# A convolution stage with ten of its sixteen blocks on TensorE, delayed copies through memory, grouped statistics, and a layer norm whose steps stand in one order

## The chip, the core and the metric

One core of a Trainium2 chip runs one program. Its engines are TensorE (PE, with its weight loads shown apart as PEld), VectorE (DVE), ScalarE (ACT), GpSimd (POOL) and SyncE (SP), each with an instruction stream of its own, and 16 DMA engines that serve the DMA queues of SP, ACT and POOL. The metric is the device time of one execution in microseconds (us), where less is better.

## The reference

A trunk of two layers (DEPTH 2, width 2048, 256 frames, float32). Each layer has a token mixer (layer 0: the Conformer convolution module, layer 1: gated linear attention) and a gated feed-forward network with a short convolution. The modulations come from a vector c by a projection. The change touches the start and layer 0's mixer:

```python
mod = (c_act @ ada_w[i] + ada_b[i]).reshape(B, N_MOD, 1, D)
h = _rms_norm(x, norm_g[i, 0]) * (1.0 + scale_m) + shift_m

def _conv_module(h, w_in, dw_w, dw_b, ln_g, ln_b, w_out):
    a, gate = jnp.split(h @ w_in, 2, axis=-1)
    z = _causal_dwconv(a * jax.nn.sigmoid(gate), dw_w, dw_b)   # CONV_WIDTH = 31 taps
    z = jax.nn.silu(_layer_norm(z, ln_g, ln_b))                # over the 2048 channels
    return z @ w_out

x = x + gate_m * _rms_norm(y, norm_g[i, 1])
```

## The kernel before

**Layout.** Channels stand on partitions, in 16 blocks of 128, and the 256 frames in the free direction; the projections into a mixer yield this layout. cout, the projection out of the mixer, yields tokens on partitions, in four columns (c) of 512 channels, from four weight tiles each. Every weight tile is 128 x 2048 (1 MB). SP loads the tiles in one list (`items`), which sets the order of the loads; `Stream` splits each into a high half on ACT (hi, L121) and a low half on DVE (lo, L123), in pieces of 1024, and three matmuls make one product: hi with the activation's high half, hi with its low half, lo with its high half (L756 to L758 in cin, L522 to L524 in cout).

**The projections of c.** adaLN tiles lie in the same list, of two kinds. For a "col" (in_adac, in_adah) PE multiplies c's columns with the tile (L364), DVE transposes the sums (L371), and PE (L378) and DVE (L381) finish. For a "row" (in_adar) DVE multiplies the tile with `cb`, a broadcast of silu(c), and sums along the row in one instruction (L350, 128 x 2048; a second small one reads the sum). `COLS_CONV`, `COLS_COUT` and `ROWS_COUT` say how many of them stand at each place of the program.

**Order.** The instructions of each engine are issued in an order that a scheduler settles at build time from the program's order and its priorities (`tc.high_priority`); `tc.issue_after` ties an instruction behind another one. An engine runs its list in that order, and so does each queue that issues DMAs.

**cin and gating.** The projection yields a and gate of a block side by side. `gather` adds the partial sums (L665) and multiplies by the sigmoid (L668 on ACT, L671 on DVE). The result zp is a block's input for the convolution.

**The convolution** starts as blocks come out of cin and goes on behind it. There are two routes. On DVE (`taps_dve`, eight blocks, two at a time) ACT makes the first tap and DVE thirty more, each a multiply-add over what is left of the frames (L685). On TensorE (`taps_pe`, the blocks in `PE_BLOCKS`) channels are split into four groups of 32. For each group an array of 128 partitions holds the 32 channels at four delays (zr): ACT copies zp behind 32 zeros (L708), PE makes each array by four matmuls with an identity (ps_late, L713), ACT copies it (L715). Then eight steps of four matmuls side by side (L730) sum all 32 delays, four at a time, by shifted views of zr and diagonal weights zt. DVE writes the first half of zt in one instruction (L724), ACT the second in 16 (L728). ACT evacuates with the bias (L733).

**Statistics.** PE sums each block over channels by a matmul with ones (`mean_add`, acc_m, L644). After twelve blocks (NA) their mean is taken as an estimate (mean_a); DVE subtracts it from each block (L631), ACT squares, PE sums (acc_v, L633). The last four are corrected for.

**Layer norm and cout.** r_ln is formed (L783 to L786: variance, clamp, root on ACT, reciprocal), every block has mu subtracted (L789), is multiplied by r_ln (L792), goes through ACT with gain, bias and Silu (L793) and is split into uc (ACT L424, DVE L425). cout (L522 to L524) multiplies these with weights; DVE multiplies the result by the gate (y, L583). The gate reaches its rows through memory: POOL's queue writes modulation columns out element by element (row<-m, L508) and reads them back as broadcast rows (gs, L512).

## Time and profile before

| what | us |
|---|---|
| median of 3 runs | 2376.75 |
| their range | 2374.56 to 2379.02 |
| the profiled execution | 2376.87 |
| its span | 2375.2 |
| first cin matmul | 29.6 |
| last gating of the convolution's input | 266.5 |
| variance (r_ln) formed | 352.4 |
| first cout matmul | 368.8 |
| last cout matmul | 463.0 |

All places in time are counted from the start of the span. The page gives busy time by engine, by line and by slices, and a chain of waits that is followed back from the last instruction. In the rows below, `L685 DVE ... out<-in ... x151 | 58.9, 460 | 0.0` reads: line of the kernel, engine, operation, tiles, shape, count, then busy us and mean ns of one, then idle time ahead of them and what ended it. TensorE's float32 matmuls leave two records for one instruction.

### The profile page before, as it was taken

To read this page: it belongs to the slowest core of one execution; us is meant where nothing else is said; L and a number is where in the kernel's file an instruction comes from. 1 tells how busy PE (TensorE), PEld (TensorE's weight loads), DVE (VectorE), ACT (ScalarE), POOL (GpSimd) and SP (SyncE) were. 2 spreads that over 40 slices of the span, in tenths; PEclk is the share of its full clock that TensorE was granted. 3 is DMA by queue.
4 is the path that set the end of the run, shared out by engine and by line. 5 is a ranking of instruction groups with operands and counts; after the bars stand their busy time and mean duration, and the time that the engine had idled before them with its cause. 6 is when DMAs were issued, how large, how long until landed. Compare 5 with 4: busy or idle time off the path is not lost.

```text
span 2375.2 us, 34238 instructions
## 1 busy us (share of the span) xinstructions
PE 2318.7 (98%) x13516; PEld 1955.8 (82%) x13516; DVE 1772.2 (75%) x2554; ACT 1212.4 (51%) x1909; POOL 16.8 (1%) x43
## 2 busy tenths in 40 slices
PE   6999998999999999999999999999999999999998
PEld 5888746788878888888878888888888888888886
DVE  3779998778878888888877877756887466645665
ACT  5334465555534554345565576655554455544543
POOL 0000000000000000000000000000000000000000
PEclk9999998999999999999999999999999999999999
DMA  9878778657799878988946756563778555555553
GB/s 387 344 311 322 299 222 309 265 216 276 291 310 348 303 279 316 362 288 298 345 174 258 283 216 227 168 227 121 286 280 275 193 190 193 189 185 196 193 199 121
DMA packets 86577, 609.30 MB, mean 257 GB/s; under 512 B 10064, under 2 KB 10128, under 8 KB 13456
## 3 DMA queue, kind: packets, MB, share of 16 engines
q1 hardware_dynamic: 84800, 601.84, 69.2%
q0 software_dynamic: 1472, 4.23, 0.6%
q8 instruction: 106, 1.74, 0.3%
q10 hardware_dynamic: 144, 1.05, 0.1%
q14 instruction: 55, 0.45, 0.1%
HBM read 604.94 MB, written 2.13 MB: 256 GB/s over the span
## 4 chain that ended last, share of the span: by engine, by line
PE 95%; DMA 2%; DVE 1%; ACT 1%; issue 0%; SPq 0%; DVEq 0%; ACTq 0%
PE ps_fb L410 14%; PE ps_fa L410 14%; PE ps_fa L412 7%; PE ps_fb L412 7%; PE ps_fo L524 7%; PE ps_fo L523 7%; PE ps_fo L522 6%; PE ps_cin L756 3%; PE ps_cin L758 3%; PE ps_r L410 2%; PE ps_cin L757 2%; PE ada L364 2%; PE ps_r L412 1%; PE ps_q L410 1%; PE ps_cout L522 1%; PE ps_k L410 1%
## 5 line engine op out<-in xcount | busy, mean ns | idle before, releaser
L123 DVE TENSOR_TENSOR lo<-raw,hi 128x1024 fp32r<-128x1024 f32 (+1 forms) x760 | 914.3, 1214 | 398.7 <-ACT hi L121 395.5
L121 ACT CAST hi<-raw 128x1024 fp32r<-128x1024 f32 (+1 forms) x760 | 784.9, 1042 | 807.4 <-PE ps_fa L410 195.4
L410 PE MATMUL ps_fa<-h,hi 128*128 128x512 f32 x1408 | 356.4, 393 | 0.4 <-ACT hn L486 0.4
L410 PE MATMUL ps_fb<-h,hi 128*128 128x512 f32 x1408 | 354.9, 392 | 0.0
L350 DVE CUSTOM_DVE_ANT_0 raw<-raw,cb 128x2048 f32<-128x2048 f32 x140 | 319.6, 2284 | 30.6 <-DMA raw<-in_adar 30.5
L410 PEld LDWEIGHTS ps_fa<-h,hi 128*128 128x128 f32 x1408 | 252.9, 189 | 45.7 <-DVE h L488 0.6
L410 PEld LDWEIGHTS ps_fb<-h,hi 128*128 128x128 f32 x1408 | 252.5, 189 | 44.2
L523 PE MATMUL ps_fo<-lo,u 128*128 128x512 f32 x704 | 274.6, 390 | 4.1 <-DVE lo L123 4.1
L524 PE MATMUL ps_fo<-hi,u 128*128 128x512 f32 x704 | 274.6, 390 | 0.0
L522 PE MATMUL ps_fo<-hi,u 128*128 128x512 f32 x704 | 273.7, 390 | 0.0
L412 PEld LDWEIGHTS ps_fa<-h,lo 128*128 128x128 f32 x1408 | 193.7, 190 | 15.1 <-DVE lo L123 0.5
L412 PEld LDWEIGHTS ps_fb<-h,lo 128*128 128x128 f32 x1408 | 193.7, 190 | 14.7
L412 PE MATMUL ps_fa<-h,lo 128*128 128x256 f32 x1408 | 198.3, 282 | 0.1
L412 PE MATMUL ps_fb<-h,lo 128*128 128x256 f32 x1408 | 198.2, 282 | 0.0
L523 PEld LDWEIGHTS ps_fo<-lo,u 128*128 128x128 f32 x704 | 132.6, 188 | 32.1 <-DVE lo L123 4.6
L756 PE MATMUL ps_cin<-h,hi 128*128 128x256 f32 x512 | 148.4, 293 | 7.3 <-ACT hi L121 7.2
L524 PEld LDWEIGHTS ps_fo<-hi,u 128*128 128x128 f32 x704 | 132.5, 188 | 27.7
L522 PEld LDWEIGHTS ps_fo<-hi,u 128*128 128x128 f32 x704 | 132.6, 188 | 27.1
L758 PE MATMUL ps_cin<-h,lo 128*128 128x256 f32 x512 | 145.2, 288 | 1.1 <-DVE lo L123 1.1
L757 PE MATMUL ps_cin<-h,hi 128*128 128x256 f32 x512 | 146.0, 287 | 0.0
L756 PEld LDWEIGHTS ps_cin<-h,hi 128*128 128x128 f32 x512 | 100.0, 196 | 21.5 <-ACT hi L121 11.8
L758 PEld LDWEIGHTS ps_cin<-h,lo 128*128 128x128 f32 x512 | 99.2, 196 | 3.2 <-issue 1.7
(240 smaller groups left out, 2697.9 us busy)
## 6 DMA issues: line engine op xcount, KB each, us to landing
raw<-in_fin SPq DMA_DIRECT2D x176, 1024.0 KB, 4.8
raw<-in_adar SPq DMA_DIRECT2D x140, 1024.0 KB, 5.6
raw<-in_fout SPq DMA_DIRECT2D x88, 1024.0 KB, 5.1
raw<-in_adac SPq DMA_DIRECT2D x44, 1024.0 KB, 5.8
raw<-in_gin SPq DMA_DIRECT2D x33, 1024.0 KB, 4.9
raw<-in_cin SPq DMA_DIRECT2D x32, 1024.0 KB, 11.1
raw<-in_cout SPq DMA_DIRECT2D x16, 1024.0 KB, 7.8
raw<-in_gv SPq DMA_DIRECT2D x16, 1024.0 KB, 4.8
```

The lines of the kernel that those rows point to most:

```text
L121: nc.scalar.copy(hi[:, :w], r[:, s : s + w])
L123: nc.vector.tensor_sub(lo[:, :w], r[:, s : s + w], hi[:, :w].bitcast(F32))
L350: V.tensor_tensor_reduce(out=r, in0=r, in1=cb, scale=1.0, scalar=0.0, op0=ALU.mult, op1=ALU.add, accum_out=mod[l, m][:, k : k + 1])
L364: nc.tensor.matmul(ps[32 * (j % 4) : 32 * (j % 4) + 32], cz[:, kt], r[:, j * n : (j + 1) * n], start=kt < 4, stop=kt >= KT - 4, tile_posit ...
L410: nc.tensor.matmul(ps, hi(k * P), act[k], start=k == 0, stop=False)
L412: nc.tensor.matmul(ps[:, :T], lo(k * P), act[k][:, :T], start=False, stop=k == nk - 1)
L522: nc.tensor.matmul(pv, ah, wh, start=kt == 0, stop=False)
L523: nc.tensor.matmul(pv, ah, wl, start=False, stop=False)
L524: nc.tensor.matmul(pv, al, wh, start=False, stop=kt == nk - 1)
L756: nc.tensor.matmul(ps[:, b], hi(o), ah, start=k == 0, stop=False)
L757: nc.tensor.matmul(ps[:, b], hi(o), al, start=False, stop=False)
L758: nc.tensor.matmul(ps[:, b], lo(o), ah, start=False, stop=k == nk - 1)
```

## The change

It has these parts.

- `PE_BLOCKS`: blocks 8 and 10 go from DVE's route to TensorE's, ten instead of eight. In odd blocks DVE writes both halves of zt (one instruction each), in even ones ACT still makes the second half in 16.
- The four-fold delayed array no longer comes from ps_late and ACT's copies. zp is written to memory by a DMA of ACT's queue, behind a pad of zeros that POOL's queue writes at the program's start (two DMAs a block: 128 x 32 and four elements). Four DMAs a block read it back as 32 x 1152 each, at four delays. They stand on POOL's queue for the first three blocks, and on ACT's for the others, there each behind the evacuation of the convolution three blocks earlier, whose buffer (zrs, three of them) it fills. For this order of partitions the host permutes the columns of the cin weights of these blocks.
- `statistics`: the sums of the first twelve blocks are taken in groups of four blocks, with matmuls of 32 columns side by side (acc_p, acc_q), the last four as before.
- Layer norm: the instructions on DVE are tied one behind the other (`queue`): three subtractions before the reciprocal, then for each block the multiplication, the low half of the block two before, the subtraction of the block three after. Tables of ACT's functions are fetched ahead.
- Layer 0's row reductions that come up from here on wait for the last of these (`after("ln")`); transposes of adaLN sums for the reciprocal (`after("r")`); four of the sixteen adaLN column tiles of this stage are put behind the statistics, and `COLS_COUT` is laid out anew.
- The start: the broadcast of c (1 MB) goes from the head of ACT's queue to SP's, behind the first cin tile; the part of the parameters that is needed early is loaded by ACT's queue, the rest later; x and the first adaLN tiles alternate on SP. The taps' array becomes smaller (128 x 512).

The diff, cut:

```diff
-PE_BLOCKS = (5, 7, 9, 11, 12, 13, 14, 15)
+PE_BLOCKS = (5, 7, 8, 9, 10, 11, 12, 13, 14, 15)
-COLS_CONV = 16
+COLS_CONV = 12
-COLS_COUT = (0, 0, 0, 1), (1, 1, 1, 1), (1, 1, 0, 0), (0, 0, 0, 0)
+COLS_COUT = (0, 0, 0, 0), (0, 1, 0, 1), (0, 1, 0, 1), (0, 0, 0, 0)
...
+    pr = const.tile([P, NPAR], F32, tag="pr", name="pr")
+    A.dma_start(out=pr[:, :C_DWB], in_=par[:, :C_DWB])
...
-        early = key[0] == "col" or key[:3] in (("row", 0, 0), ("row", 0, 3))
+        early = key[0] == "col" or key[:2] == ("row", 0) and key[2] != 5
...
-    early_cols = list(cols[:COLS_CONV])
-    fillc(COLS_CONV)
+    early_cols = list(cols[: COLS_CONV + 4])
+    fillc(COLS_CONV + 4)
...
+    def after(key):
+        return tc.issue_after(apool[key].ins) if key in apool else ExitStack()
+
     def ada_row(key, r):
 
         _, l, m, k = key
-        V.tensor_tensor_reduce(out=r, in0=r, in1=cb, scale=1.0, scalar=0.0, op0=ALU.mult, op1=ALU.add,
-                               accum_out=mod[l, m][:, k : k + 1])
+        with after("ln") if l == 0 else ExitStack():
+            V.tensor_tensor_reduce(out=r, in0=r, in1=cb, scale=1.0, scalar=0.0, op0=ALU.mult, op1=ALU.add,
+                                   accum_out=mod[l, m][:, k : k + 1])
...
+            with after("tok"):
+                nc.tensor.matmul(ps[32 * (j % 4) : 32 * (j % 4) + 32], cz[:, kt], r[:, j * n : (j + 1) * n],
...
+                with after("r"), tc.high_priority(SPLIT_FIRST):
+                    V.transpose(out=tr, in_=ps[:, h : h + T])
...
-    st.load(1)
     for t in range(2):
+        st.load(t + 2)
         for c in range(4):
             nc.sync.dma_start(out=X[t][c], in_=x[t, :, c * 512 : (c + 1) * 512])
-    nc.sync.dma_start(out=pr, in_=par)
-    st.load(4)
+    st.load(5)
+    nc.sync.dma_start(out=cb, in_=cvec.to_broadcast([P, D]))
+    nc.sync.dma_start(out=pr[:, C_DWB:], in_=par[:, C_DWB:])
...
-            on_dve, on_pe, ready, order = [], [], [], []
-            zps = [cm.tile([P, 32 + T], F32, tag=f"zp{i}", name=f"zp{i}", bufs=1) for i in range(2)]
-            for zp in zps:
-                G.memset(zp[:, :32], 0.0)
+            on_dve, on_pe, ready, done, order, fetched, convolved = [], [], [], [], [], [], [0]
+
+
+            W = 32 + T
+            zrs = [cm.tile([P, 4 * W], F32, tag=f"zr{i}", name=f"zr{i}", bufs=1) for i in range(3)]
+            zds = [dram.tile([4 + P * W], F32, tag=f"zd{i}", name=f"zd{i}", bufs=1) for i in PE_BLOCKS]
+            zero = cm.tile([P, 32], F32, tag="zero", name="zero", bufs=1)
+            G.memset(zero, 0.0)
...
+            def sums(few, all_, n, tiles):
+
+
+                mm = None
+                for i, z in reversed(list(enumerate(tiles))):
+                    if n < NA:
+                        with tc.issue_after(mm.ins) if mm else ExitStack(), tc.high_priority(SPLIT_FIRST):
+                            mm = nc.tensor.matmul(acc[few][32 * i : 32 * i + 32], ones[:, :32], z, start=n == 0, stop=n == NA - 4,
+                                                  tile_position=(0, 32 * i))
+                    else:
+                        mm = nc.tensor.matmul(acc[all_], ones, z, start=all_ == "m" and n == NA, stop=n == KT - 1)
+                return mm
...
+                sqs = [Y[j][:, 0] for j in js]
+                for sq, j in zip(sqs, js):
+                    V.tensor_sub(sq, zs[j], mean_a)
+                    A.activation(sq, sq, AF.Square)
+                apool["sqs"] = sums("q", "v", n, sqs)
+                squared.extend(js)
...
-                        on_pe.append((j, zp, z))
+                        A.dma_start(out=zds[len(order)][4:].rearrange("(p c) -> p c", c=W)[:, 32:], in_=zp)
+                        order.append(j)
+                        fetch()
...
+            def fetch():
+
+                n = len(fetched)
+                if n < min(len(order), convolved[0] + 3):
+                    for i in range(4):
+                        (G if n < 3 else A).dma_start(out=zrs[n % 3][32 * i : 32 * i + 32],
+                                    in_=zds[n][1 + i : 1 + i + P * W].rearrange("(n c) -> n c", c=4 * W))
+                    fetched.append(n)
+                    on_pe.append((order[n], zrs[n % 3]))
+
             def taps_pe():
 
 
                 while on_pe:
-                    j, zc, z = on_pe.pop(0)
-                    zp = zps[len(order) % 2]
-                    order.append(j)
-                    A.copy(zp[:, 32:], zc)
-                    zr = cm.tile([P, 4, 28 + T], F32, tag="zr", name="zr")
-                    for b in range(4):
-                        pr4 = pp["ps"].tile([P, 512], F32, tag="ps", name=f"ps_late{j}_{b}")[:, : 28 + T]
-                        for i in range(4):
-                            nc.tensor.matmul(pr4[32 * i : 32 * i + 32], ident[:, 32 * b : 32 * b + 32], zp[:, 4 - i : 32 + T - i],
-                                             start=True, stop=True, tile_position=(0, 32 * i))
-                        A.copy(zr[:, b], pr4)
-                        yield None
+                    j, zr = on_pe.pop(0)
                     ps = pp["ps"].tile([P, 2 * T], F32, tag="ps", name=f"ps_conv{j}")[:, :T]
-                    c0 = KT * CW + j * 32
-                    w = tp[:, c0 : c0 + 32].rearrange("p (j a) -> p a j", a=8)
+                    w = tp[:, j * 32 : j * 32 + 32].rearrange("p (j a) -> p a j", a=8)
                     for a in range(8):
                         if a % 4 == 0:
-                            if a == 0:
+                            if a == 0 or j % 2:
...
-                            nc.tensor.matmul(ps[32 * b : 32 * b + 32], zt[:, a % 4, b], zr[:, b, 28 - 4 * a : 28 - 4 * a + T],
+                            nc.tensor.matmul(ps[32 * b : 32 * b + 32], zt[:, a % 4, b], zr[:, b * W + 32 - 4 * a : b * W + 32 - 4 * a + T],
                                              start=a == 0, stop=a == 7, tile_position=(0, 32 * b))
                         yield None
-                    A.activation(z, ps, AF.Identity, bias=pc(C_DWB + j))
+                    A.activation(zs[j], ps, AF.Identity, bias=pc(C_DWB + j))
+                    convolved[0] += 1
...
+                if s == 2:
+                    for zd in zds:
+                        G.dma_start(out=zd[4:].rearrange("(p c) -> p c", c=W)[:, :32], in_=zero)
+                        G.dma_start(out=zd[:4].unsqueeze(0), in_=zero[:1, :4])
...
+            gap = early_cols[COLS_CONV:]
+            del early_cols[COLS_CONV:]
+            while len(squared) < KT:
+                if early_cols:
+                    st.upto(("col",) + early_cols.pop(0), False)
+                conv(pe, taps_pe, 8)
+                conv(dve, taps_dve, 9)
+                statistics()
+                done.extend(ready)
+                ready.clear()
+            assert not early_cols
...
+            line = []
+
+            def queue(f, *args):
+
+                with tc.issue_after(line[-1].ins) if line else ExitStack():
+                    line.append(f(*args))
+
+            def center(j):
+                if j < KT:
+                    queue(V.tensor_sub, zs[j], zs[j], mu)
+
+            def low(j):
+                if j >= 0:
+                    queue(V.tensor_sub, us[j][:, T:], zs[j], us[j][:, :T].bitcast(F32))
+
+            with tc.high_priority(SPLIT_FIRST):
+
+
+                queue(V.scalar_tensor_tensor, part_a, acc["m"], 1.0 / D, part_a, ALU.mult, ALU.add)
+                queue(V.tensor_add, mu, mean_a, part_a)
+                A.activation(part_a, part_a, AF.Square)
+                queue(V.scalar_tensor_tensor, r, acc["v"], 1.0 / D, part_a, ALU.mult, ALU.subtract)
+                queue(V.tensor_scalar_max, r, r, 0.0)
+                root = A.activation(r, r, AF.Sqrt, bias=epsb)
+                with tc.issue_after(root.ins):
+                    warm(AF.Silu, part_a)
+                for j in range(3):
+                    center(j)
+                queue(V.reciprocal, r, r)
+                apool["r"] = line[-1]
+                for j in range(KT):
+                    queue(V.tensor_mul, zs[j], zs[j], r)
+                    A.activation(zs[j], zs[j], AF.Silu, bias=pc(C_LNB + j), scale=pc(C_LNG + j))
+                    us.append(hpool.tile([P, 2 * T], F32R, tag="h", name=f"uc{j}"))
+                    A.copy(us[j][:, :T], zs[j])
+                    low(j - 2)
+                    center(j + 3)
+                low(KT - 2)
+                low(KT - 1)
+                apool["ln"] = line[-1]
+            apool["tok"] = apool["sqs"]
+            st.upto(("col",) + gap[-1], False)
...
+    late = np.concatenate([dw[::-1], np.zeros((32 - CW, D), dw.dtype)]).reshape(8, 4, KT, 4, 32)[:, ::-1]
+    late = late.transpose(1, 4, 2, 3, 0).reshape(P, KT, 32)
+    taps[:, PE_BLOCKS] = late[:, PE_BLOCKS]
...
+    ci[PE_BLOCKS,] = ci[PE_BLOCKS,].reshape(-1, 2, P, KT, 4, 32).swapaxes(-1, -2).reshape(-1, 2, P, KT, P)
```

How the order of the engines' instructions moves, at the three places that matter. pairJ is block J's buffer, loN the low half of weight tile N, rawN a loaded tile, m03 the shift of the feed-forward network's modulation.

On PE, behind the last cin matmul, before:

```order
L364 MATMUL ada028_2630<-raw75_2470,cz_80 32x512 x4
L644 MATMUL acc_m0_2867<-pair0_301,ones_74 128x256
L644 MATMUL acc_m0_2867<-pair1_316,ones_74 128x256
L713 MATMUL ps_late5_0_2872<-zp0_176,ident_85 32x284 x4
L713 MATMUL ps_late5_1_2878<-zp0_176,ident_85 32x284 x4
L713 MATMUL ps_late5_2_2884<-zp0_176,ident_85 32x284 x4
L713 MATMUL ps_late5_3_2890<-zp0_176,ident_85 32x284 x4
L364 MATMUL ada0212_2862<-raw76_2547,cz_80 32x512 x4
L730 MATMUL ps_conv5_2896<-zr_2871,zt_2897 32x256 x12
```

and in the change:

```order
L372 MATMUL ada028_2682<-raw75_2520,cz_84 32x512 x4
L773 MATMUL ps_conv5_2922<-zr0_182,zt_2923 32x256 x9
L372 MATMUL ada0212_2917<-raw76_2598,cz_84 32x512 x4
L773 MATMUL ps_conv5_2922<-zr0_182,zt_2923 32x256 x7
L773 MATMUL ps_conv5_2922<-zr0_182,zt_2941 32x256 x16
```

The delayed copies are gone, and block 5's convolution stands right behind cin.

On DVE, where layer norm begins, before:

```order
L350 ISA raw98_3824,m03_103<-raw98_3824,cb_83 128x2048
L350 ISA m03_103 128x1
L783 SCALAR_TENSOR_TENSOR r_ln_3885<-acc_v_3612,part_a_181 128x256
L789 TENSOR_TENSOR pair0_301<-pair0_301,mu_3882 128x256
L784 TENSOR_SCALAR r_ln_3885<-r_ln_3885 128x256
L789 TENSOR_TENSOR pair1_316<-pair1_316,mu_3882 128x256
```

and in the change:

```order
L831 SCALAR_TENSOR_TENSOR r_ln_3663<-acc_v_3646,part_a_198 128x256
L391 TENSOR_TENSOR m04_107<-adas044_3777,pr_74 128x4
L831 TENSOR_SCALAR r_ln_3663<-r_ln_3663 128x256
L831 TENSOR_TENSOR pair0_316<-pair0_316,mu_199 128x256
L831 TENSOR_TENSOR pair1_331<-pair1_331,mu_199 128x256
L831 TENSOR_TENSOR pair2_346<-pair2_346,mu_199 128x256
L831 RECIPROCAL r_ln_3663<-r_ln_3663 128x256
L831 TENSOR_TENSOR pair0_316<-pair0_316,r_ln_3663 128x256
L831 TENSOR_TENSOR pair3_361<-pair3_361,mu_199 128x256
```

The row reduction ahead of r_ln is gone, and the first multiplication stands behind three subtractions, not sixteen.

On DVE, behind the last low half of layer norm, before:

```order
L425 TENSOR_TENSOR uc15_3985<-pair15_626,uc15_3985 128x256
L350 ISA raw104_4118,m03_103<-raw104_4118,cb_83 128x2048
L350 ISA m03_103 128x1
L123 TENSOR_TENSOR lo105_0_4197<-raw105_4120,hi105_0_4196 128x1024
L123 TENSOR_TENSOR lo105_1024_4201<-raw105_4120,hi105_1024_4200 128x1024
L583 TENSOR_TENSOR y01_00_4176<-ps_cout_0_0_3992,gs0_3988 128x512
```

and in the change:

```order
L831 TENSOR_TENSOR uc15_3764<-pair15_641,uc15_3764 128x256
L122 TENSOR_TENSOR lo100_1024_3949<-raw100_3832,hi100_1024_3948 128x1024
L357 ISA raw96_3771,m03_106<-raw96_3771,cb_87 128x2048
L357 ISA m03_106 128x1
L122 TENSOR_TENSOR lo103_0_4006<-raw103_3934,hi103_0_4005 128x1024
L357 ISA raw97_3773,m03_106<-raw97_3773,cb_87 128x2048
```

In the change the first of the sixteen row reductions of m03 stands here; before, the one shown is the sixth.

107 lines of the change are left out of this document (41 added, 66 removed).

## The prediction

> **What bounds the kernel now.** I read the chain of waits first, then a table of the first layer's stages, then the engines inside the stages that the change touches. The page says:
>
> ```profile
> span 2375.2 us, 34238 instructions
> PE 95%; DMA 2%; DVE 1%; ACT 1%; issue 0%; SPq 0%; DVEq 0%; ACTq 0%
> ```
>
> TensorE carries the chain over the whole span, but 95% is an average. The stages, cut where the events stand (columns: length, then busy time of PE, PEld, DVE, ACT, POOL, then granted clock, DMA share, GB/s):
>
> ```profile
> 0.00:29.60 29.60, 9.41 (x88) 4.68 (x88) 5.01 (x20) 14.88 (x37) 1.50 (x12) 0.96 0.94 372
> 266.50:352.40 85.90, 85.80 (x1055) 47.69 (x1056) 82.14 (x203) 51.04 (x182) 1.33 (x1) 1.00 0.73 265
> 352.40:368.80 16.40, 2.71 (x12) 0.20 (x8) 16.39 (x41) 7.92 (x15) 2.15 (x4) 0.68 0.94 200
> 368.80:463.00 94.20, 93.73 (x424) 74.28 (x421) 76.58 (x88) 48.88 (x76) 0.00 (x0) 0.98 0.82 320
> ```
>
> They are: the start up to the first cin matmul; the convolution's stage after the last gating, to the instruction that forms layer norm's variance (r_ln, 352.40); layer norm; the cout projection. The projection into the convolution (29.6 to 266.5) and all behind 463 keep their work. In the convolution's stage DVE is busy 82.14 of 85.90 us, so DVE sets its pace; what it does there:
>
> ```profile
> L685 DVE SCALAR_TENSOR_TENSOR pair<-pair,tp 128x241 f32<-128x241 f32 (+19 forms) x151 | 58.9, 460 | 0.0
> L631 DVE TENSOR_TENSOR sq<-pair,mean_a 128x256 f32<-128x256 f32 x16 | 6.4, 419 | 1.4 <-PE acc_v L633 1.3
> L123 DVE TENSOR_TENSOR lo<-raw,hi 128x1024 fp32r<-128x1024 f32 x4 | 4.8, 1212 | 0.0
> L724 DVE TENSOR_TENSOR zt<-tp,mask 128x512 f32<-128x512 f32 x7 | 4.7, 678 | 0.0
> L350 DVE CUSTOM_DVE_ANT_0 raw<-raw,cb 128x2048 f32<-128x2048 f32 x2 | 4.6, 2290 | 0.0
> ```
>
> Mean times overlap at their ends: 151 taps keep DVE busy 58.9 us, so one more costs 0.39 us. PE's records there also show no gap, but a record runs from issue, so I price PE by starts:
>
> ```profile
> 309.26 1.04 PE L364 MATMUL ada<-raw,cz 128*32 128x512 f32 x8
> 310.12 0.61 PE L730 MATMUL ps_conv<-zr,zt 128*32 128x256 f32 x8
> 310.55 2.10 PE L713 MATMUL ps_late<-zp,ident 128*32 128x284 f32 x32
> 312.47 1.06 PE L730 MATMUL ps_conv<-zr,zt 128*32 128x256 f32 x5
> 315.67 3.23 PE L730 MATMUL ps_conv<-zr,zt 128*32 128x256 f32 x56
> 318.71 1.04 PE L364 MATMUL ada<-raw,cz 128*32 128x512 f32 x8
> 324.59 1.56 PE L644 MATMUL acc_m<-pair,ones 128*128 128x256 f32 x6
> 326.08 2.35 PE L730 MATMUL ps_conv<-zr,zt 128*32 128x256 f32 x36
> ```
>
> An instruction leaves two records. From start to start, a block's delayed copies (32 records) take 1.92 us, 56 convolution records 3.04 (a block, 64, takes 3.5), an adaLN block of 8 records 0.86, a statistics record 0.25. Eight blocks of each, the 142 adaLN records of this row of that line, and 64 statistics records
>
> ```profile
> 266.50:352.40 85.90, 29.21 (x142) 7.04 (x144) 1.00 0.73 265
> ```
>
> make 28 + 15 + 15 + 16 = 74 us: PE is the close second.
>
> **Convolution's stage.** By the order, between the last gating and r_ln, DVE now issues 91 taps (60 fewer: -23.4 us), no row reduction (-4.6), 14 tap masks (zt) for 7 (+4.7, at 0.67), with the low halves, squares and transposes as before. 82.1 - 23.3 = 58.8, about 60 us. PE: ten blocks, 35; no copies, 0; 12 adaLN blocks and a rest, 13; statistics in groups: six groups of twelve blocks, each four matmuls side by side like a step of the convolution (0.43), and ten full ones at 0.5, 8; small sums, 4. Again 60 us. ACT loses the copies into zr and zp and 64 of its 128 small zt copies (128 take 31.4 us), against 38 DMA issues at 0.41 us:
>
> ```profile
> L715 ACT COPY zr<-ps_late 128x284 f32<-128x284 f32 x32 | 12.5, 390 | 2.4 <-PE ps_late L713 2.1
> L728 ACT ACTIVATE zt<-mask,tp 128x32 f32<-128x32 f32 x128 | 31.4, 319 | 6.7 <-DMA tp<-in_taps 6.7
> L708 ACT COPY zp<-pair 128x256 f32<-128x256 f32 x8 | 3.2, 405 | 0.8 <-DVE pair L671 0.7
> 0.81 0.41 ACTq L740 DMA_DIRECT2D cb<-in_cvec  x1
> ```
>
> So 12.5 + 3.2 + 15.7 go and 15.6 come: ACT, at 51 of 86, stays under the others. Where nothing overlaps there is a tail: last convolution, evacuation, mean, four squares, sum, about 6 us. 60 + 6, and 2 for two engines that are now equally full: r_ln 68 us after the last gating instead of 85.9, **-18**. Bounds: 61 (the tail hidden) to 77 (a late fetch, next), -25 to -9.
>
> The new path is one fetch of 590 KB in four DMAs, which nothing in this trace does. From below, 256 KB rows in gs; from above, 1 MB weight loads in the crowded stretch and the 2,048 single elements of row:
>
> ```profile
> raw<-in_adar SPq DMA_DIRECT2D x5, 1024.0 KB, 15.1
> gs<-row POOLq DMA_DIRECT2D x4, 256.0 KB, 7.2
> row<-m POOLq DMA_DIRECT2D x1, 8.0 KB, 16.7
> ```
>
> Fetch n+3 is issued on ACT's queue behind the evacuation of block n, so the ten blocks run in three rounds of fetch L plus 4 us (convolution and evacuation), behind some 8 us until the first block is done and before 5 for the last block's tail: r_ln at 25 + 3L. L = 7.2 gives 47, hidden under the 68; L = 14 just meets it; L = 16.7 gives 75. I take L below 14, since a fetch is nearest in size to halfway between 256 KB and 1 MB and the rows it copies are 4.6 KB long. What stands behind the issuing ACT is only its own next copies. The adaLN blocks, all of them prefetched weights, keep their order between convolution steps.
>
> The Trainium skill (DMA: Bandwidth & Descriptors, Anatomy of one DMA) gives 2.0 us plus bytes over 436 GB/s per DMA on the POOL path. By that the fetch alone would be an estimated 3.4 us, and r_ln would be set by the engines; the row's 7.2 us for 256 KB is well over that formula's estimate of 2.6, so I go by the row.
>
> **Layer norm and cout.** These are priced together, from r_ln to cout's end, now 463.0 - 352.4 = 110.6 us:
>
> ```profile
> 352.40 0.42 DVE L783 SCALAR_TENSOR_TENSOR r_ln<-acc_v,part_a 128x256 f32<-128x256 f32 x1
> 353.28 3.44 DVE L789 TENSOR_TENSOR pair<-pair,mu 128x256 f32<-128x256 f32 x10
> 366.96 2.29 DVE L350 CUSTOM_DVE_ANT_0 raw<-raw,cb 128x2048 f32<-128x2048 f32 x1
> 368.83 0.80 PE L522 MATMUL ps_cout<-hi,uc 128*128 128x512 f32 x1
> ```
>
> In the new order only three subtractions precede the reciprocal instead of 16 all before the first multiplication, and the first block's halves are ready some 7 us behind r_ln, not 16.4. PE's pace in cout is this:
>
> ```profile
> 380.00:390.00 10.00, 10.00 (x46) 8.28 (x45) 10.00 (x13) 7.81 (x15) 0.00 (x0) 1.00 0.89 319
> 388.08 2.36 DVE L123 TENSOR_TENSOR lo<-raw,hi 128x1024 fp32r<-128x1024 f32 x2
> L522 PE MATMUL ps_cout<-hi,uc 128*128 128x512 f32 x128 | 50.8, 402 | 0.0
> L583 DVE TENSOR_TENSOR y<-ps_cout,gs 128x512 f32<-128x512 f32 x8 | 5.4, 688 | 8.8 <-ACT junk L430 6.5 <-PE ps_cout L524 2.3
> ```
>
> 3 x 128 matmuls at 10/44 (46 records less two of adaLN) are 87.4 us; four adaLN blocks instead of seven add 3.4: PE alone would be done at r_ln + 99. But DVE cannot feed it. In these 10 us it is busy throughout already. All 16 of layer 0's row reductions of shift now wait for the last layer norm instruction, where 13 stood in cout before (one was in layer norm, two earlier). DVE's list up to the low half that cout's last column needs first: layer norm to the last uc with six weight halves among it, 45 x 0.344 + 6 x 1.18 + 4 = 26.5; 16 x 2.29 = 36.6; 16 more halves, 18.9; six y, 3.7: r_ln + 86. The last column's 96 matmuls are 21.8: r_ln + 108, with PE idle some 9 us on the way. The gain of layer norm is thus given back in cout: **-2**. Bounds: -11 (PE alone: the reductions find gaps) to +4 (the idle time halves the clock for a while; layer norm's row shows a clock of 0.68).
>
> **Start.** The 1 MB broadcast moves behind the first cin block, the parameters are split: bytes ahead of that block fall from 9.06 to 7.25 MB, which at the start's 372 GB/s is -4.8 us. Against it stand 1,290 writes of 128 or 16 bytes at the head of POOL's queue (the zero pads). The nearest row is the scatter:
>
> ```profile
> 353.00:361.00 8.00, 0.27 (x2) 0.00 (x0) 8.00 (x22) 3.83 (x6) 0.00 (x0) 0.84 0.93 65
> L121 ACT CAST hi<-raw 128x1024 fp32r<-128x1024 f32 (+1 forms) x98 | 101.6, 1063 | 104.7 <-DMA raw<-in_cin 37.7 <-PE ps_cin L757 32.1 <-PE ps_cout L524 27.8
> ```
>
> 65 GB/s at a share of 0.93: 2,048 elements cost about 7 us of transfer, so 1,290 cost up to 4.5; by bytes alone 0.4. The projection behind it also waits for its own loads (ACT, which splits them, 37.7 us in all), which can eat an earlier start. Of -4.8 + (0.4 to 4.5) I take **-2** (-4.4 to +3).
>
> The Trainium skill (same page, Specifications) says that transfers under 512 bytes are read-modify-write and miss the line rate; the scatter's row bears it out, and by it the start would lean to the upper end, -0.3.
>
> **Sum.** -18 - 2 - 2 = -22: span 2353.2. The profiled run took 2376.87, 1.67 over its span and 0.12 over the runs' median of 2376.75; so **2355**.
>
> **Rivals.**
>
> *The memory route sets the pace.* Fetches share their engines with weight loads. The stage moves 22.8 MB now (85.9 x 265); with 5.9 MB fetched and in 68 us that would be 422 GB/s, what only the best 10 us of cout reach:
>
> ```profile
> 420.00:430.00 10.00, 10.00 (x46) 8.29 (x45) 10.00 (x10) 4.80 (x6) 0.00 (x0) 1.00 1.02 424
> 430.00:440.00 10.00, 10.00 (x42) 7.57 (x41) 8.48 (x10) 3.91 (x3) 0.00 (x0) 1.00 0.91 361
> 361.00:366.00 5.00, 0.00 (x0) 0.00 (x0) 5.00 (x17) 3.94 (x10) 2.15 (x4) 0.50 0.83 308
> ```
>
> For it: also the 15.1 us row, and row, which is issued before r_ln and would meet the last fetches. Against: much of the 22.8 MB is for cout and can land later. L = 16.7 gives r_ln at 75, and 1 more for a fetch that meets the scatter: -10 - 4 = 2363. Chance 0.20.
>
> The Trainium skill (SBUF — State Buffer, two separate sides) warns that a POOL-queue DMA starves while DVE holds a shared port. That bears on the first three fetches only. Here gs, on that queue and issued in the last of the stretches above, landed in 7.2 us with DVE busy 5.00 of 5.00 us, so I give it no more.
>
> *Cout is bound by PE.* If reductions fill DVE's waits for PE's results, cout ends at r_ln + 99, 9 us earlier than forecast: 2346. For it: DVE's sum misses PE by only 9 us. Against: DVE is busy 10.00, 10.00 and 8.48 us of the three 10 us windows of cout shown, with fewer reductions than now come. Chance 0.15.
>
> *Slower.* The same loop with a fetch so late that it costs more than all else saves. It decides from 25 + 3L > 90, L about 22 us; three rounds at 28 give r_ln at 109, +23 - 4 = +19: 2396. For it: each fetch is four DMAs behind ACT's in-order work and behind weight loads already in the same engines. Against: no load in the trace took as long; the worst medians are 15 to 17. Chance 0.10.
>
> **How the numbers follow.** Forecast 0.55, within 2348 to 2362; the memory route 0.20, cout on PE 0.15, slower 0.10. 0.2% of 2376.75 is 4.75 us, about what this kernel's timing can tell from none. The forecast and cout on PE are faster whole; of the memory route 0.14 are, with 0.05 the same and 0.01 slower. Faster 0.84, same 0.05, slower 0.11. The range runs from cout's -11 with a middle convolution (2340) to the memory route with a bad start (2371).
>
> **What would show it.** Right: DVE's taps 180 in all, r_ln 64 to 72 us behind the last gating; first cout matmul about 7 us behind r_ln; PE idle in the middle of cout waiting for low halves with DVE busy without a gap on reductions; first cin matmul about 27.6. The fetch's time to landing under 14 us. Wrong: PE waiting for zr from a DMA between convolution blocks, a late first cin, or a cout without idle PE.

## The result and the profile after

The changed kernel takes 2393.22 us (median of 4 runs, 2390.81 to 2396.65), the kernel before 2377.6 beside it: a ratio of 1.0068, 95% interval 1.0055 to 1.008. It is slower by 0.7%, where 0.9% faster was forecast. Its profiled execution is the longest of its four, with a span of 2394.9 us, 19.7 over the span before.

The same cut of the span for the kernel after (columns as in the prediction); the convolution's stage, from the last cin matmul to r_ln, stands in three pieces:

```profile
0.00:27.10 27.10, 10.35 (x88) 4.89 (x88) 4.46 (x18) 10.88 (x26) 12.16 (x31) 1.00 0.95 365
264.60:318.00 53.40, 42.62 (x531) 19.98 (x533) 47.97 (x115) 11.79 (x40) 0.00 (x0) 0.87 1.00 320
318.00:338.00 20.00, 2.35 (x44) 1.09 (x36) 0.90 (x3) 0.50 (x2) 1.22 (x1) 0.66 1.01 202
338.00:361.50 23.50, 22.98 (x312) 16.73 (x316) 9.77 (x26) 16.69 (x58) 2.16 (x4) 0.92 0.36 119
361.50:368.30 6.80, 3.74 (x56) 1.04 (x45) 6.76 (x17) 4.94 (x10) 0.00 (x0) 1.00 0.71 255
368.30:483.10 114.80, 100.77 (x447) 76.97 (x440) 92.01 (x120) 51.40 (x81) 0.00 (x0) 0.90 0.77 300
```

From mark to mark, before and after:

| stretch | before | after | difference |
|---|---|---|---|
| start to the first cin matmul | 29.6 | 27.1 | -2.5 |
| cin, to its last matmul | 236.7 | 237.5 | +0.8 |
| from there to r_ln | 86.1 | 96.9 | +10.8 |
| r_ln to the first cout matmul | 16.4 | 6.8 | -9.6 |
| cout | 94.0 | 114.8 | +20.8 |
| the rest | 1912.4 | 1911.8 | -0.6 |

The start and layer norm gained what was forecast. The loss sits in the convolution's stage and in cout. (The prediction counted from 266.5, where the last cin matmul ends; the last gating itself starts at 268.0 there and at 266.6 after. From here on stages are counted from the start of that gating: 84.4 us to r_ln before, 94.9 after.)

In the middle piece four engines stand almost still for 20 us while DMA is busy for all of it and moves only 202 GB/s. The timeline after, of ACT, POOL and PE there:

```profile
318.50 1.22 POOL L519 DMA_DIRECT2D row<-m  x1 [78.04 <-DVE m L516]
322.00 15.92 ACTq L751 DMA_DIRECT2D zr<-zd  x4
337.97 3.51 ACT L771 ACTIVATE zt<-mask,tp 128x32 f32<-128x32 f32 x16 [18.80 <-DMA zr<-zd]
338.35 4.16 PE L773 MATMUL ps_conv<-zr,zt 128*32 128x256 f32 x39 [17.99 <-ACT zt L771]
```

and what was issued in these 20 us, with the time from issue to landing:

```profile
raw<-in_cout SPq DMA_DIRECT2D x1, 1024.0 KB, 9.1
zr<-zd ACTq DMA_DIRECT2D x4, 144.0 KB, 13.1
row<-m POOLq DMA_DIRECT2D x1, 8.0 KB, 15.5
```

The element by element write of row, which before was issued at 345.71 and ran mostly inside layer norm, now leaves at 318.5, between the last fetches. ACT, issuing the fetch of block 14, stands at its four DMAs for 16 us; the tap masks of block 12 stand behind them on ACT, and PE waits for these. Three of the four DMAs leave by 323.3. The fourth leaves at 337.62, right behind the landing of a cout weight load that SP had issued at 310.10 and that took 27.5 us:

```profile
310.10 0.33 SPq L96 DMA_DIRECT2D raw<-in_cout  x1
raw<-in_cout SPq DMA_DIRECT2D x1, 1024.0 KB, 27.5
337.62 0.31 ACTq L751 DMA_DIRECT2D zr<-zd  x1
```

In this program the DMAs of SP's and ACT's queues signal their landing by the same eight semaphores, and each issue first waits on the semaphore that it will use. So a fetch on ACT can wait for a weight load on SP. POOL's DMAs have eight others.

In cout, the waits after name late loads, and in a part of it DMA is full:

```profile
ACT hi L120 <- DMA raw<-in_cout: 19.5, 3, 13.6
DVE raw L357 <- DMA raw<-in_adar: 6.3, 5, 2.7
PE ada L372 <- DMA raw<-in_adac: 5.8, 1, 5.8
```

```profile
420.00:440.00 20.00, 9.95 (x45) 5.51 (x44) 13.77 (x15) 3.11 (x6) 0.00 (x0) 0.76 0.99 392
```

SP's queue shows one reason why they are late: after, it issues no load between 334.6 and 362.57 (what it then waited for is PE's last matmul, at 362.55, on a kept column tile),

```profile
308.07 26.50 SPq L96 DMA_DIRECT2D raw<-in_cout  x4
362.57 2.90 SPq L96 DMA_DIRECT2D raw<-in_adar  x4
```

where the kernel before issues four row tiles from 335.69 on:

```profile
335.69 11.70 SPq L97 DMA_DIRECT2D raw<-in_adar  x4
```

### The profile page after: what moved, and what is told of

It is laid out like the page before. It is cut to its first block, busy times and chain, and to the rows that moved or that the text cites. A ratio compares the mean times of both kernels' runs of the same rounds, so it can differ in the third digit from the quotient of the medians.

```text
span 2394.9 us, 33947 instructions
## 1 busy us (share of the span) xinstructions
PE 2311.0 (96%) x13392; PEld 1950.9 (81%) x13392; DVE 1755.4 (73%) x2502; ACT 1186.5 (50%) x1807; POOL 33.2 (1%) x74
## 4 chain that ended last, share of the span: by engine, by line
PE 91%; DMA 5%; DVE 2%; ACT 1%; issue 1%; SPq 0%; DVEq 0%; ACTq 0%
PE ps_fb L421 14%; PE ps_fa L421 13%; PE ps_fa L423 7%; PE ps_fb L423 7%; PE ps_fo L534 6%; PE ps_fo L533 6%; PE ps_fo L535 6%; PE ps_cin L804 3%; PE ps_cin L806 2%; PE ps_r L421 2%; PE ps_cin L805 2%; DMA raw<-in_adar 2%; PE ada L372 1%; PE ps_r L423 1%; PE ps_q L421 1%; PE ps_k L421 1%
## 5 line engine op out<-in xcount | busy, mean ns | idle before, releaser
L533 PEld LDWEIGHTS ps_fo<-hi,u 128*128 128x128 f32 x704 | 132.6, 188 | 27.4
```

Of the source, the lines that this page charges most:

```text
L533: nc.tensor.matmul(pv, ah, wh, start=kt == 0, stop=False)
```

## The experiments

All ratios are to the kernel before, run beside each on the same chip. "Stage" is from the last gating to r_ln, "cout" from r_ln to cout's last matmul, both of the profiled execution. That execution lies up to 4.2 us off its kernel's median, so smaller differences in these two columns are not told from noise.

| kernel | ratio, 95% interval | stage | cout |
|---|---|---|---|
| before | 1 | 84.4 | 110.4 |
| the change | 1.0068 (1.0055 to 1.008) | 94.9 | 121.6 |
| write of row late | 1.0034 (1.002 to 1.0049) | 86.9 | 120.3 |
| no column tiles kept | 1.0073 (1.0056 to 1.009) | 94.9 | 117.8 |
| both | 1.0046 (1.0031 to 1.0061) | 93.2 | 116.6 |
| both, rows free | 1.0031 (1.0021 to 1.0041) | 93.3 | 108.2 |
| ... fetches on POOL's queue | 0.9998 (0.9989 to 1.0007) | 90.3 | 108.7 |
| ... fetches of a quarter's size | 0.9969 (0.9957 to 0.9982) | 66.0 | 126.3 |
| ... copies by PE and ACT | 0.9993 (0.9983 to 1.0002) | 91.9 | 105.2 |
| the change, write of row flat | 1.0036 (1.0023 to 1.0049) | 86.2 | 121.9 |
| flat, four early rows | 1.0026 (1.0016 to 1.0037) | 98.5 | 109.2 |
| ... copies by PE and ACT | 0.9995 (0.9985 to 1.0004) | 91.7 | 107.8 |
| ... fetches of a quarter's size | 0.9932 (0.9917 to 0.9948) | 72.7 | 109.0 |
| put together | 0.9952 (0.9937 to 0.9966) | 81.5 | 107.5 |

### The write of row late, and kept column tiles

The first edit, in `gate_rows`:

```diff
-        V.tensor_mul(mod[l, gate], mod[l, gate], pc(C_NG + l * 64 + which * KT, KT))
+        with after("r") if (l, which) == (0, 1) else ExitStack():
+            V.tensor_mul(mod[l, gate], mod[l, gate], pc(C_NG + l * 64 + which * KT, KT))
```

> One edit to the changed kernel: the multiplication that ends the gate's column form (L516) waits for layer norm's reciprocal, so that the element by element write of row leaves POOL's queue behind r_ln and not at 318.5 us, between the convolution's last fetches. Theory (the write holds the DMA engines, so that fetches and ACT, which waits to issue them, come late): the 18 us in which PE waits for the tap masks of block 14 go, r_ln moves from 361.5 to 343 to 346, the time from 2393 to about 2375. Rival (fetches are late on their own, whatever else moves, because DMA is full): r_ln stays at 356 or later and the time above 2388.

Measured: 2385.01 us, the ratio half of what it was above 1, the stage 8 us shorter. The theory's direction holds; its size is half. PE's long wait (for the masks of block 12, not 14 as the expectation has it) falls from 18.0 to 8.4 us and does not go, and ACT waits at a fetch for a weight load, as above:

```profile
PE ada L372 <- DMA raw<-in_adac: 11.4, 3, 5.7
PE ps_conv L774 <- ACT zt L772: 8.4, 1, 8.4
```

```profile
ACT zt L772 <- DMA raw<-in_cout: 9.6, 1, 9.6
```

So the write, where it stood, cost 8 us, and something else holds the stage at 87 where 68 was forecast.

The second edit takes the loop's split of the column tiles out:

```diff
-            gap = early_cols[COLS_CONV:]
-            del early_cols[COLS_CONV:]
...
-            st.upto(("col",) + gap[-1], False)
```

> One edit to the changed kernel: the four adaLN column tiles that are kept for the gap behind the statistics are used inside the convolution's stage, as before the change. Theory (these tiles hold all four buffers of their pool from about 300 until 357 us, so the row tiles behind them load only from 362 and cout's weights behind those come late): the loads go on before 362, the stretch from r_ln to cout's end falls from 121.6 to 108 to 112 us, r_ln itself moves by 0 to +4 (3.4 us of matmuls return to the stage), the time to about 2383 to 2388. Rival (cout is long because DVE has 16 row reductions in it): the stretch stays at 119 to 122 and the time at 2393 to 2397.

Measured: 2393.37 us, no change in time, as the rival has it. SP's next load leaves at 342.46 and not at 362.57, but cout is only 3.8 us shorter in the profile. The kept tiles alone are not the cause.

```profile
342.46 16.72 SPq L96 DMA_DIRECT2D raw<-in_adar  x4
```

With both edits:

> Both edits: the late write of row, and no column tiles kept for the gap. If both theories hold, the gains add: r_ln at 343 to 349, cout's end 108 to 112 us behind it, time 2362 to 2370. If only the write mattered, about 2375; if the loads were late only because of the write, the same as with the late write alone.

Measured: 2385.95 us, as with the late write alone. The gains do not add: the four column tiles return to a stage that grows from 86.9 to 93.2 us.

The tie of the row reductions taken off on top of both:

```diff
-        with after("ln") if l == 0 else ExitStack():
+        with ExitStack():
```

> Both edits, and the row reductions of layer 0 no longer wait for the last instruction of layer norm (L357 without its tie): by the order five of the sixteen then stand ahead of or inside layer norm. Theory (DVE is the bound in cout, so reductions done in the convolution's stage, where DVE waits anyway, shorten cout): r_ln and first cout matmul up to 6 us later than with both edits, cout's end 3 to 8 us earlier, time 3 to 6 us below that of both edits. Rival (PE and the loads set cout's pace): the same time as with both edits within 2 us, or longer by the reductions that stand in layer norm, up to 7 us.

Measured: 2384.38 us; the interval overlaps that of both edits. cout is 8.4 us shorter in the profile, but this profiled execution is 4.2 us below its kernel's median, so the time shows no clear gain.

### What fills the convolution's stage

Three edits on that last kernel. First, the queue of the fetches:

```diff
-                        (G if n < 3 else A).dma_start(out=zrs[n % 3][32 * i : 32 * i + 32],
+                        G.dma_start(out=zrs[n % 3][32 * i : 32 * i + 32],
```

> The kernel with the late write of row, no column tiles kept for the gap and free row reductions, and one edit more: all ten fetches of the delayed copies stand on POOL's queue, none on ACT's. Theory (ACT waits to issue a fetch until weight loads of SP's queue have landed, and its tap masks and evacuations stand behind that): ACT's waits for zr and weight loads (24 us in the stage) go, r_ln comes 8 to 15 us earlier than 358.8 and the time falls from 2384 to 2370 to 2377. Rival (the DMA engines are full in this stage, whichever queue issues): r_ln within 4 us of 358.8, the time 2381 to 2388.

Measured: 2380.2 us, ratio 0.9998: faster than its base by 0.3%. The time lies between the two expectations, 0.8 below the rival's; r_ln, from 358.8 to 355.3, moves as little as the rival has it. ACT's waits for DMA do go, but PE now waits for column tiles, and these land later (15.3 us after issue, 10.8 in the base):

```profile
PE ada L372 <- DMA raw<-in_adac: 14.3, 4, 8.8
PE ps_cout L534 <- ACT uc L860: 12.9, 1, 12.9
PE adas L388 <- DVE adat L380: 3.5, 1, 3.5
```

The wait changed its place with the queue. That speaks for full DMA engines, with ACT's in-order wait as the smaller part.

Second, the size of a fetch. The number of DMAs stays, and three quarters of the channels of the ten blocks are not convolved:

```diff
-                        (G if n < 3 else A).dma_start(out=zrs[n % 3][32 * i : 32 * i + 32],
-                                    in_=zds[n][1 + i : 1 + i + P * W].rearrange("(n c) -> n c", c=4 * W))
+                        (G if n < 3 else A).dma_start(out=zrs[n % 3][32 * i : 32 * i + 32, :W],
+                                    in_=zds[n][1 + i : 1 + i + P * W].rearrange("(n c) -> n c", c=4 * W)[:, :W])
```

> The same base (late write of row, no kept tiles, free row reductions), with fetches on ACT's queue as there, but each DMA of a fetch brings only 288 of its 1152 columns; the rest of zr holds zeros, so three quarters of the channels of the ten blocks get no convolution. The number of DMAs and their waits stay, 4.4 MB of fetched bytes become 1.1 MB. Theory (DMA full): r_ln comes 6 to 12 us earlier than 358.8, fetches land in 4 to 5 us. Rival (ACT's waits for a place behind weight loads): r_ln moves by less than 4 us, since these waits do not depend on a fetch's size.

Measured: 2373.56 us. The stage falls from 93.3 to 66.0 us, more than twice what was expected, and to within 2 us of the forecast's 60 + 6 + 2. The same 60 us of both kernels, first the base, then the quarter:

```profile
265.00:325.00 60.00, 43.49 (x556) 20.39 (x548) 47.44 (x114) 11.85 (x40) 0.00 (x0) 0.89 1.01 321
```

```profile
265.00:325.00 60.00, 58.44 (x868) 33.23 (x857) 56.09 (x138) 28.25 (x97) 0.00 (x0) 1.00 0.90 321
```

With the full fetches DMA is busy 1.01 of the time and PE 43.49 us; with the quarter DMA is at 0.90 and PE works 58.44. (Both move 321 GB/s: with small fetches SP gets further with its weights.) Column tiles land in 7.4 us instead of 10.8, cout's in 7.2 instead of 17.0. This shows what the stage lost: the engines' sums were right, and the bytes of the fetches, on DMA engines shared with weight loads, were the loss, since the number of DMAs is the same. Whether the bytes cost it by DMA time alone, or by the lists that wait for late landings as well, it does not separate. Of the 27 us some 15 arrive (0.62% by the ratios), as cout grows to 126.3: there the late write stands far into cout, and y waits for it.

```profile
DVE y L595 <- DMA zr<-row: 16.5, 1, 16.5
```

That is a fault of this experiment's late write, which the flat write below avoids.

Third, no memory route at all: the copies by PE (ps_late) and ACT as before the change, two buffers of zr, the host's permutation undone.

> The same base with ten blocks on PE, but the delayed copies made by PE and ACT as before the change, with no write of zp, no zero pads and no fetch, and two buffers of zr instead of three. PE's sum for the stage by starts is 35 + 19 + 13 + 8 + 4 = 79 us. Theory (the memory route costs more than the copies it saves): r_ln at 80 to 87 us behind the last gating, against 93.3 with the memory route, and the time 2371 to 2378. Rival (the memory route is the gain, and PE full of copies is worse): r_ln at 93 or later, the time above 2384.

Measured: 2378.4 us, faster than its base by 0.4%. The route costs more than the copies that it replaces, as the theory has it; the stage, 91.9 us, stays 5 above the theory's range, with PE busy nearly throughout. Six row reductions are in it here, three in the base.

### The write of row, flat

The gate's column is turned by a small matmul, and 16 rows of 512 bytes are written:

```diff
-            G.dma_start(out=row.rearrange("k p -> p k"), in_=mod[l, gate])
+            nc.tensor.matmul(pt, mod[l, gate], ident, start=True, stop=True)
+            A.copy(flat, pt)
+            G.dma_start(out=row, in_=flat)
```

> The changed kernel with one edit: the gate's column form (128 x 16) is turned by PE into 16 rows of 128 and written to row in 16 pieces of 512 bytes, not in 2,048 of 4 bytes. Nothing else waits or moves by intent (PE's small matmul stands at the head of cout). Theory (the element writes hold the DMA engines at 318 to 334 us): r_ln moves from 361.5 to 346 to 354, the time from 2393 to 2378 to 2386, at least as much as with the late write (2385). Rival (the write only happened to stand there): 2390 or more.

Measured: 2390.0 us beside 2380.2 for the kernel before, so a ratio of 1.0036 against 1.0068: the same gain as the late write, with r_ln at 351.7, inside the theory's range, and a stage of 86.2. (The kernel before stands at 2377.3 to 2380.5 from one group of runs to the next, so kernels of different groups are compared by ratios; by its absolute time alone this one would meet the rival.) But the edit changes more than the size of the pieces. The small matmul stands at the head of cout, and so the write leaves late as well, at 361.64 where the change has 318.50:

```profile
361.64 0.49 POOL L524 DMA_DIRECT2D row<-flat  x1 [123.02 <-ACT flat L523]
```

Both edits take the write out of the stage, both win the same 8 us, and both leave the stage at 86 to 87. Whether 16 rows would have done no harm at 318.5 is not shown.

On top of it, four of the sixteen row tiles were put into the convolution's stage, and no column tile kept:

```diff
+    early_rows = list(rows[:4])
+    for _ in range(4):
+        fillc(4)
+        fill(1)
...
+                    if len(early_cols) % 4 == 0:
+                        st.upto(("row",) + early_rows.pop(0), False)
```

> The flat write, no column tiles kept for the gap, and four of the sixteen row tiles used inside the convolution's stage, one behind each four column tiles; the other twelve still wait for layer norm's end. The memory route stays. Theory (in the convolution's stage DMA is the bound: four more MB cost it 11 us there, in cout it frees them): r_ln 85 to 95 us behind the last gating, cout's end 100 to 108 us behind r_ln, time 2372 to 2382. Rival (DVE's waits take the four reductions in for nothing, and DMA keeps up): r_ln at 80 or less, time below 2368.

Measured: 2386.06 us, ratio 1.0026. The stage grows by 12 us to 98.5 and cout shrinks by 13 to 109.2. The theory has the direction of both parts (four more tiles at a full DMA, about 11 us), but stage, cout and time all lie past its ranges. The matmuls of the four column tiles are back in the stage too, and in cout four reductions fewer and eight tiles fewer to load come together; what each gives is not separated. PE's waits in the stage are almost all for loads:

```profile
PE ada L375 <- DMA raw<-in_adac: 20.5, 6, 8.4
PE adas L391 <- DVE adat L383: 2.3, 1, 2.3
```

Then the same without the memory route:

> As the kernel with flat write and four early rows, but with the delayed copies by PE and ACT instead of the memory route, ten blocks on PE. Theory (without 590 KB a block DMA is not the bound; PE is, with 79 us by starts): r_ln 82 to 88 us behind the last gating, cout's end 100 to 105 us behind r_ln, time 2364 to 2374, so below both the changed kernel and the kernel before. Rival (the memory route is no slower than PE's copies once the write is flat): the same time as with the memory route within 3 us.

Measured: 2378.17 us, ratio 0.9995: 0.3% below the memory route, but not below the kernel before. The stage is 91.7 us where 82 to 88 was expected, and the time misses its range too. PE is busy nearly throughout:

```profile
265.00:325.00 60.00, 56.92 (x842) 33.65 (x836) 54.20 (x123) 28.59 (x93) 0.00 (x0) 1.00 0.84 316
```

Counted from start to start, the 640 records of the convolution take 46.5 us of the stage, where the sum of 79 has 35, and the copies 21.8 where it has 19. Why, the trace doesn't tell.

And with the memory route at a quarter of the bytes:

> As the kernel with flat write and four early rows, memory route on ACT's queue, but each DMA of a fetch brings 288 of its 1152 columns (three quarters of the channels of ten blocks get no convolution). Theory (the engines' sums of the forecast, 60 us each and a tail of 6, hold when DMA is not full): r_ln 64 to 70 us behind the last gating. For cout: if DVE's list is its bound, now four reductions (9 us) shorter, its end is 97 to 103 us behind r_ln and the time 2350 to 2360; if the supply of weights is, its end stays at 450 to 458 in the span and the time at 2366 to 2374.

Measured: 2363.77 us, ratio 0.9932. The stage is 72.7 us (four row tiles are in it), above the 64 to 70 expected, and 26 below the same kernel with full fetches. With the write and the rows mended, the plan of the change is thus worth 0.7% with fetches of a quarter's size, and loses 0.3% with full ones. cout, at 109.0, is neither at DVE's 97 to 103, nor does it end in 450 to 458 (447.1).

### A version that beats both

Nine blocks on PE, the memory route for the first three alone, whose fetches run during cin; for the others the matmuls and copies of the kernel before stand where the diff is cut:

```diff
-PE_BLOCKS = (5, 7, 8, 9, 10, 11, 12, 13, 14, 15)
+PE_BLOCKS = (5, 7, 8, 9, 11, 12, 13, 14, 15)
...
+                        if j in PE_BLOCKS[:3]:
+                            A.dma_start(out=zds[len(order)][4:].rearrange("(p c) -> p c", c=W)[:, 32:], in_=zp)
+                            order.append(j)
+                            fetch()
+                        else:
+                            on_pe.append((j, zp))
...
+                    if j not in PE_BLOCKS[:3]:
+                        zc, zr, zp = zr, zrs[convolved[0] % 3], zps[0]
+                        A.copy(zp[:, 32:], zc)
+                        for b in range(4):
...
+                            A.copy(zr[:, b * W + 4 : b * W + W], pr4)
```

> A kernel put together from what the runs showed: nine blocks on PE (10 goes back to DVE), the memory route for the first three alone, whose fetches run during cin, PE's and ACT's copies for the other six, the flat write of row, four row reductions in the convolution's stage, no column tiles kept for the gap, layer norm's order and the start as in the changed kernel. Sums: PE 31.5 + 11.5 + 13 + 8 + 4 = 68 us, DVE 60 + 11.7 + 9.2 for the early reductions = 81 us, no fetch in the stage. Theory (DMA full of fetches was the loss): r_ln 80 to 86 us behind the last gating, cout's end 103 to 108 us behind r_ln, time 2362 to 2372, below the kernel before by 0.2 to 0.7%. Rival (with DVE at 81 us this stage is where it was, and cout gives the rest back): 2374 to 2380.

Measured: 2369.33 us, ratio 0.9952 (0.9937 to 0.9966): 0.5% faster than the kernel before, 1.2% faster than the change (by the ratios). The stage is 81.5 us, cout 107.5. What each of the edits gives in it was not run apart. In most of the stage PE and DVE are both busy, and DMA is not full:

```profile
263.00:300.00 37.00, 35.32 (x536) 21.60 (x535) 36.50 (x86) 12.92 (x37) 0.00 (x0) 1.00 0.86 326
300.00:340.00 40.00, 38.90 (x502) 21.91 (x502) 38.15 (x87) 22.34 (x73) 0.00 (x0) 1.00 0.80 289
```

## Why the prediction was wrong

**What bounds the kernel** (DVE, then PE, in the convolution's stage) held: where fetches are small, the stage runs at 66.0 us, and in 60 us of it DVE is busy 56.09 and PE 58.44.

**The convolution's stage, -18: this term failed**, at +10.8. The counts were right (91 taps on DVE behind the last gating, 35.5 us) and so were the sums of the two engines. The step that failed is the one that priced a fetch as a time to landing, 25 + 3L, and put the DMA engines' own sum among the rivals with a fifth of the chance. It should have been a third sum beside DVE's 60 and PE's 60. The shares of the DMA queues over 60 us (265 to 325) give its prices, first with the memory route (the kernel "both, rows free"; q1 SP's loads, q10 ACT's queue: packets, MB, share), then without it ("flat, four early rows" with copies by PE and ACT):

```profile
q1 hardware_dynamic: 2192, 15.90, 79.9%
q10 hardware_dynamic: 1226, 3.30, 20.5%
```

```profile
q1 hardware_dynamic: 2580, 18.82, 83.6%
```

83.6% of 60 us for 18.82 MB is 2.7 us of all 16 engines per MB of weights; 20.5% for 3.30 MB is 3.7 per MB of fetch. The stage after has 17 weight tiles (13 column tiles, 4 of cout: 17.8 MB, 48 us), seven fetches behind the last gating (4.1 MB, 15 us) and the write of row (8 us by the two edits that take it out of the stage): 71 us, more than either engine; beside fetches a MB of weights costs 3.0 (79.9% for 15.90 MB), and then it is 77. The trace shows this full stretch. From the last gating DMA is full for 71.4 us, to 338:

```profile
266.60:338.00 71.40, 42.97 (x548) 20.16 (x543) 47.15 (x114) 11.87 (x41) 1.22 (x1) 0.81 1.01 287
```

PE did only 42.97 us of its work in it. What stands behind the last fetches and masks came after: PE is busy 22.98 of the last 23.5 us, with DMA at 0.36. In the forecast this tail was 6 us. The likely reason that PE got so little done beside the full DMA is the lists: ACT, PE and SP each wait in order for whatever lands last. How much each of these waits takes was not separated. The rival of the memory route had the right cause and a size that was too small: it gave r_ln 7 us over the forecast's 68 (and 1 for a meeting with the write). It held 422 GB/s against the 424 that cout reaches with weight loads alone; with fetches among them a full DMA moved 320.

**The meeting of the write and the last fetches** was named in that rival, at 1 us. It cost 8. The write was priced at a meeting with one fetch; what counted is that all loads beside it slow down, and that ACT stands at the issue of a fetch's four DMAs for 16 us, with the masks of block 12 behind them. The prediction had asked what stands behind the issuing ACT, and named "only its own next copies". ACT's half of the masks, for the blocks with an even number, was what PE waited for.

**The latency of a fetch.** L was taken below 14. One DMA landed in 7.3 us in the median (13.1 in the stretch of the write), but L is a fetch of four: from the first issue to the last landing the ten fetches took 5.3 to 21.0 us, 12.2 in the median, and three of them more than 14. Still the loop of three buffers was not what decided: PE's waits in the stage name masks and column tiles, and never zr. The "slower" rival (L of 22 or more) names ACT's in-order work and the weight loads, which the runs bear out, but prices them by that loop; that its 2396 comes within 3 us of the measured time is luck. The Trainium skill's formula for one DMA on POOL's path (DMA: Bandwidth & Descriptors, Anatomy of one DMA; 2.0 us plus bytes over 436 GB/s) gives an estimate of 2.3 us for one of 144 KB. The trace comes near it only where DMA is not full: the DMAs of the last fetch of the kernel with the late write, on ACT's queue and at a DMA share of 0.39 (333 to 340), landed in 2.9 us.

```profile
zr<-zd ACTq DMA_DIRECT2D x4, 144.0 KB, 2.9
```

**Layer norm and cout, -2: this term failed too**, at +11.2. Its first half was right: the first cout matmul came 6.8 us behind r_ln, where 7 was said. "PE idle on the way" was right in sign. The reason given, DVE's list up to r_ln + 108, does not reach the 121.6 that came: DVE itself waits for row tiles, ACT for weights. (The sum for PE alone, 7 + 87.3 + 3.4, is 98 and not 99; nothing hangs on it.) The step left out is what the kept column tiles and the tie do to the loads. They leave SP no buffer to load into for 28 us, while DMA is at 0.36; behind r_ln SP then has 30 weight tiles of layer 0 to issue (16 row, 10 cout, 4 column) where it had 25 before, and cout runs into a full DMA (0.99 at 392 GB/s). In the forecast's terms: the wait for a held buffer was the missing wait. What the loads and what DVE's reductions take of the +11.2 is not separated. With 16 reductions in cout and 30 tiles to issue cout takes 120.3 to 121.9 us over the runs; with 16 and 26, 116.6 to 117.8; with 12 and 22 to 24, 107.5 to 109.2. What still holds cout at 107 to 109, where DVE's list with twelve reductions and PE's 98 both end earlier, is not settled; in the last version PE waits 5.6 us for uc, and from 420 to 440 it is busy 15.75 of 20 with DMA at 0.97.

**The start, -2: right**, at -2.5, of which 1.7 are left at the last cin matmul. It lies midway between the bounds (-4.4 and -0.3) for the small zero writes, whose own cost was not measured apart: cin starts at 25.5 us in both kernels without them, and at 25.5 to 27.4 in the ten that have all of them. The Trainium skill's rule on transfers under 512 bytes (same page, Specifications), which leant to -0.3, is not borne out in full there. For the write of row it fits: 2,048 pieces of 4 bytes land in 15.5 us, 16 pieces of 512 bytes in 1.6, though at another place, with DMA less full.

```profile
row<-flat POOLq DMA_DIRECT2D x1, 8.0 KB, 1.6
```

**Rivals.** That a DMA on POOL's queue starves while DVE holds a shared port (the Trainium skill, SBUF — State Buffer, two separate sides) shows in no run: with all fetches on that queue the kernel was faster than with ACT's. The fetches landed in 11.0 us there, against 7.3 in the base; with DMA full, that doesn't tell.

## What to carry to other kernels

Where a change relieves two engines that are almost equally full, sum the third resource too: for DMA that is bytes times the busy share that the same bytes take now, for everything that must land in the shortened stage, not a latency per transfer. A tile that waits for permission to be used holds a buffer, and the queue that loads into it stops; look for what that queue would have loaded next. Before a transfer is put on a compute engine's queue, list what stands behind its issue on that engine, and what the issue itself waits for: here it was a semaphore shared with another queue's loads.

## What was not expected of the hardware

- In the 20 us that begin with the write of 8 KB in 2,048 elements, DMA is busy at 1.01 and moves only 202 GB/s, and the DMAs of a fetch take 13.1 us instead of 7.3. The time shows in the other queues: the write's own (q0) has 1.0% of these 20 us, and SP's loads (q1) take 4.9 us per MB, where they take 2.7 to 3.0 in the stretches above.

```profile
q1 hardware_dynamic: 452, 3.29, 80.2%
q0 software_dynamic: 48, 0.01, 1.0%
```

- Fetches in rows of 4.6 KB cost 3.7 us of all DMA engines per MB, where weight rows of 8 KB beside them cost 3.0, and 2.7 without them. That the length of the rows is the reason is not shown.
- Taking 3.3 MB of fetches out of a stage with full DMA (4.4 to 1.1 MB) shortened it by 26 to 27 us in two pairs of kernels, though by the price above they fill only some 12 us. That lists which wait in order make the rest of it is the likely reason, and was not measured apart.
